# Moving the SBUF start addresses of four groups of tiles by fillers of 32 and 64 bytes, in a four-mixer decoder trunk

## The chip, the cores and the metric

The kernel runs on one core of one Trainium2 chip. The metric is the device time of one execution in microseconds (us). Three runs of the kernel before gave 3079.8, 3082.81 and 3086.07 us; the median is 3082.81 us. The profile is of one more execution, which took 3081.34 us.

## The reference, cut to what matters

The program computes two residual layers over 1024 tokens of 1024 channels in float32. Each layer has a mixer and a gated feed-forward part (ConvFFN) with a hidden width of 2816. The even layer's mixer is a gated DeltaNet with four heads beside a multi-scale pooling; the odd layer's mixer is a dilated sliding-window attention with three groups of eight heads.

```python
for i in range(DEPTH):                       # DEPTH = 2
    mod = (cs @ ada_w[i] + ada_b[i])[:, None, :]
    sh_m, sc_m, g_m, sh_f, sc_f, g_f = jnp.split(mod, 6, axis=-1)
    hm = rms_norm(x, norm_mix[i]) * (1.0 + sc_m) + sh_m
    y = even_mixer(hm, ...) if i % 2 == 0 else odd_mixer(hm, ...)
    x = x + g_m * y
    hf = rms_norm(x, norm_ffn[i]) * (1.0 + sc_f) + sh_f
    x = x + g_f * conv_ffn(hf, ffn_w_up[i], ffn_conv_w[i], ffn_conv_b[i], ffn_w_down[i])
```

## The kernel before, in words

**Split products.** The large products run in the rounded type float32r, one pass each. A weight tile of 128 partitions x 512 float32 (2 KiB in each partition) comes by DMA into `raw` or `wr`; ScalarE copies it into `whi` (the rounded weight) and VectorE or GpSimd writes the rest, weight minus rounded weight, into `wlo`. Activations are split in the same way into `hh` and `hl` or `oh` and `ol`. `mm3` (lines 204 to 208) then adds three matmuls into PSUM: high by high (L206), high weight by activation rest (L207), weight rest by high activation (L208). Here the weight block of 128 columns is stationary and 512 (at the very end 256) columns of activation move. In the odd layer's projections (`tproj`, L1354 to L1356) it is the other way round: a 128-column slice of `hh` or `hl` is stationary and 512 columns of `whi` or `wlo` move. In a profile row such as `sp<-oh,whi` the name behind the arrow is the moving operand, and the one behind the comma the stationary operand.

**Pools.** SBUF tiles come from pools, laid out one behind the other in the address space of a partition: `cst` (constants), `pw` (`raw` 4 buffers, `whi` 9, `wlo` 9), `pb` (24 buffers of 4 KiB, the large tiles: `x`, `hh`, `hl`, `oh`, `ol`, `xr`, `wr`, `v`, `sb`, `big` and others), `pt` (8 buffers `t2k` of 2 KiB and small ones), and one pool per stage: `pe` for the even mixer, `pf0` and `pf1` for the feed-forward parts, `po` for the odd mixer. Buffers of one tag follow each other at multiples of 32 bytes, and nearly all tiles of 512 bytes and more have sizes that are multiples of 128, so all buffers of such a tag share the start's remainder modulo 128 (`stg` and `ld` of the odd mixer, 2080 and 3120 bytes, do not). `fill(pool, bytes)` allocates a tile that no instruction uses, so that what follows in the pool starts later.

**Order.** The order of the instructions on each engine is the order of the Python program. Generators `weave` a chain of dependent small steps with dense matmul work. Semaphores guard every buffer. No planner chooses by address. SP issues nearly all DMAs, a few come from GpSimd and ScalarE.

The stages in time: about 0 to 540 us even mixer, to 1260 us its feed-forward part (from 985 us on the down projection), to about 2375 us odd mixer, to the end its feed-forward part.

Of the kernel before, what the change touches and what calls it, by code (L numbers as in the profile page):

```python
# [34 lines left out]
def trunk(ctx, tc, x, c, ada_w, ada_b, norm_mix, norm_ffn, ev_w_in, ev_w_out, gdn_conv_w,  # L35
# [6 lines left out]
    pw = pool("pw")  # L42
    pb = pool("pb")
# [8 lines left out]
    def nm(s):  # L52
        n_ids[0] += 1
        return f"{s}_{n_ids[0]}"
# [13 lines left out]
    def raw_tile():  # L68
        return pw.tile([P, HALF], F32, tag="raw", name=nm("raw"), bufs=4)
# [4 lines left out]
    def fill(pl, size):  # L74

        pl.tile([P, size // 4], F32, name=nm("fill"))
# [100 lines left out]


    lo_eng = [nc.gpsimd]
    last_w = [None]  # L180

    def split(dst_hi, dst_lo, src, eng):
        nc.scalar.activation(dst_hi, src, AF.Copy)  # L183
        eng.tensor_tensor(out=dst_lo, in0=src, in1=dst_hi, op=ALU.subtract)  # L184

    def granule(src, shape=None):
        raw = raw_tile()
        last_w[0] = nc.sync.dma_start(raw if shape is None else raw.rearrange(shape[0], **shape[1]), src)
        hi = pw.tile([P, HALF], F32R, tag="whi", name=nm("whi"), bufs=9)
        lo = pw.tile([P, HALF], F32R, tag="wlo", name=nm("wlo"), bufs=9)  # L190
        split(hi, lo, raw, lo_eng[0])
        return hi, lo

    def unit_c(w, c0):

        blocks = []
        for g in range(0, KT, 4):
            hi, lo = granule(w[g * P:(g + 4) * P, c0:c0 + P].rearrange("(k p) c -> p k c", p=P),
                             ("p (k c) -> p k c", dict(k=4)))
            blocks += list(zip(blk4(hi), blk4(lo)))  # L200
        return blocks
# [18 lines left out]
    def update(rows, hid, gate, xt, order, wide=False, done=None):  # L220

        wb = []
        for r in rows:
            g = [granule(r[:, q * HALF:(q + 1) * HALF]) for q in range(2)]
            wb.append([(a, b) for hi, lo in g for a, b in zip(blk4(hi), blk4(lo))])
        n = len(rows)
        ps = None
        for o, hf in order:
            s = HS[hf]
            if wide:  # L230
                ps = mm_ps() if hf == 0 else ps
                p = ps[:, s]
            else:
                p = s_ps()
            for i in range(n):
                mm3(p, wb[i][o], hid[i][hf], i == 0, i == n - 1)
                if i < n - 1:
                    yield 3 * MM
            if not wide:
                nc.vector.scalar_tensor_tensor(out=xt[o][:, s], in0=p, scalar=gate[:, o:o + 1], in1=xt[o][:, s],  # L240
                                               op0=ALU.mult, op1=ALU.add)
            elif hf:
                nc.vector.scalar_tensor_tensor(out=xt[o], in0=ps, scalar=gate[:, o:o + 1], in1=xt[o],
                                               op0=ALU.mult, op1=ALU.add)
            if done:
                done(o, hf)
            step_back()
            yield 3 * MM
# [192 lines left out]
    def even():  # L441
# [7 lines left out]
        zs, res = {}, {}  # L449

        with tc.tile_pool(name="pe", bufs=1) as pe:
            fill(pe, 64)

            def et(tag, bufs, shape=(P, HALF)):
                return tmp(tag, shape, bufs, pl=pe)
# [262 lines left out]
            def dense():  # L718
# [37 lines left out]
                with tc.issue_after(last_w[0].ins):  # L756
                    o01 = [[granule(osp[i][:, s]) for s in HS] for i in range(2)]
                    res["x"] = reload(xs[0])
# [328 lines left out]
    def ffn(l, xt, h, vec, acc, vec_next):  # L1087
        gate = mod[l][:, 40:48]
        wu, wd = ffn_w_up[l], ffn_w_down[l]
        with tc.tile_pool(name=f"pf{l}", bufs=1) as pf:  # L1090
            fill(pf, 64)

            def taps(t, src, j, dst, frm):

# [195 lines left out]
    def odd(xt, h, vec, acc):  # L1290
# [3 lines left out]
        spill(xs[1], xt)  # L1294
        lo_eng[0] = nc.vector
        with tc.tile_pool(name="po", bufs=1) as po:
            fill(po, 64)

            def et(tag, bufs, shape=(P, HALF), dt=F32):
                return tmp(tag, shape, bufs, dt, pl=po)  # L1300
# [397 lines left out]
    with tc.tile_pool(name="pa", bufs=1) as pa[0]:  # L1698
        xt, h, vec, acc = even()
        xt, h, vec, acc = ffn(0, xt, h, vec, acc, lambda: norm_vec(1, 0))  # L1700
    xt, h, vec, acc = odd(xt, h, vec, acc)
    ffn(1, xt, h, vec, acc, None)


# [27 lines left out]
```

## Time and profile before

| | |
|---|---|
| median of three runs | 3082.81 us (3079.8 to 3086.07) |
| profiled execution | 3081.34 us, its span from first to last instruction 3079.6 us |
| TensorE matmul busy | 2967.4 us, 96% of the span, 14346 matmuls |
| TensorE weight load busy | 2446.9 us, 79% |
| VectorE, ScalarE, GpSimd busy | 2018.0, 1074.1, 972.2 us (66%, 35%, 32%) |
| DMA queue q1 (the SP queue carries nearly all of it) | 300.55 MB, 31.0% of 16 engines |
| mean granted TensorE clock | 0.986 |

Matmuls are pipelined: the duration of one (0.39 us for 512 columns) overlaps the next, and its end is modelled. What sets TensorE's pace is the distance from one start to the next, which the timeline shows. A busy share of 96% therefore says that TensorE hardly idles; it says nothing on how fast it runs.

### The profile page before, as it was taken

The page shows a single profiled execution, that of the slowest core. Times are in us where ns is not written, and L with a number is a line of the kernel's source. Part 1 is how long each engine was busy: PE and PEld are TensorE (multiplying, and loading weights), DVE is VectorE, ACT ScalarE, POOL GpSimd, SP SyncE. Part 2 cuts the span into 40 slices and gives each one's busy share as a digit, 9 for nine tenths or more (in the row PEclk, how much of TensorE's full clock was granted, in tenths as well). Part 3 has the DMA queues.
Part 4 walks back from the last instruction along what each step waited for, and adds up shares of the span by engine and source line. Part 5 has one row for each costly group of instructions (what it writes and reads, how often), then busy time and mean ns, then how long its engine had stood idle before and what let it go on. Part 6 is the DMA issues. An engine that isn't in the chain of part 4 may idle for free.

```text
span 3079.6 us, 40200 instructions
## 1 busy us (share of the span) xinstructions
PE 2967.4 (96%) x14346; PEld 2446.9 (79%) x14346; DVE 2018.0 (66%) x3877; ACT 1074.1 (35%) x2170; POOL 972.2 (32%) x727
## 2 busy tenths in 40 slices
PE   6999999899999899999999999999999899999999
PEld 4777878678888777788888878888877788888888
DVE  7877745987777877754445646354687877776554
ACT  4434422433333211323333333324343433333210
POOL 4412323555555543200000010000022655555540
PEclk8999999999999999999999999999999999999999
DMA  7523323253323753221313242313243222224321
GB/s 248 145 63 99 96 91 121 72 158 110 110 86 106 240 164 114 106 86 61 106 61 114 65 149 72 115 37 117 68 163 114 85 89 83 82 82 168 110 90 59
DMA packets 275010, 331.46 MB, mean 108 GB/s; under 512 B 27411, under 2 KB 194426, under 8 KB 274810
## 3 DMA queue, kind: packets, MB, share of 16 engines
q1 hardware_dynamic: 266810, 300.55, 31.0%
q0 software_dynamic: 7040, 25.17, 2.4%
q10 hardware_dynamic: 960, 3.18, 0.3%
q8 instruction: 113, 1.85, 0.2%
q14 instruction: 87, 0.71, 0.1%
HBM read 251.82 MB, written 77.00 MB: 107 GB/s over the span
## 4 chain that ended last, share of the span: by engine, by line
PE 72%; DVE 7%; DMA 3%; issue 2%; POOL 1%; ACT 1%; SPq 0%; POOLq 0%; DVEq 0%; ACTq 0%
PE sp L206 11%; PE sp L207 11%; PE sp L208 11%; PE mm L1356 8%; PE mm L1354 8%; PE mm L1355 8%; PE mm L206 3%; PE mm L207 3%; PE mm L208 3%; PE sp L1550 2%; PE sp L1506 2%; PE sp L1386 1%; DVE ada_acc L276 1%; PE sp L1539 1%; DMA raw<-in_ada_w_dram 1%
## 5 line engine op out<-in xcount | busy, mean ns | idle before, releaser
L1354 PE MATMUL mm<-whi,hh 128*128 128x512 f32 x1152 | 482.7, 419 | 0.0
L1356 PE MATMUL mm<-whi,hl 128*128 128x512 f32 x1152 | 452.7, 393 | 0.0
L1355 PE MATMUL mm<-wlo,hh 128*128 128x512 f32 x1152 | 451.6, 392 | 0.0
L184 POOL TENSOR_TENSOR wlo<-raw,whi 128x512 fp32r<-128x512 f32 x190 | 257.0, 1367 | 544.5 <-ACT whi L183 463.8
L183 ACT ACTIVATE whi<-raw 128x512 fp32r<-128x512 f32 x334 | 208.4, 630 | 389.6 <-PE sp L207 163.0
L240 DVE SCALAR_TENSOR_TENSOR xr<-sp,mod,xr 128x512 f32<-128x512 f32 x336 | 248.0, 747 | 135.6 <-PE sp L208 135.2
L206 PE MATMUL sp<-oh,whi 128*128 128x512 f32 (+1 forms) x832 | 315.6, 379 | 20.2 <-DVE xr L240 14.2
L207 PE MATMUL sp<-ol,whi 128*128 128x512 f32 (+1 forms) x832 | 311.1, 374 | 0.0
L208 PE MATMUL sp<-oh,wlo 128*128 128x512 f32 (+1 forms) x832 | 311.0, 374 | 0.0
L206 PE MATMUL mm<-hh,whi 128*128 128x512 f32 x736 | 299.6, 407 | 8.8 <-DVE ft L1098 6.8
L207 PE MATMUL mm<-hl,whi 128*128 128x512 f32 x736 | 294.0, 399 | 3.2 <-POOL hl L377 1.6
L208 PE MATMUL mm<-hh,wlo 128*128 128x512 f32 x736 | 293.1, 398 | 0.0
L184 POOL TENSOR_TENSOR wlo<-t2k,whi 128x512 fp32r<-128x512 f32 x160 | 228.8, 1443 | 159.0 <-ACT whi L183 120.7
L1451 POOL DMA_DIRECT2D vd<-v x24 | 17.6, 735 | 771.9 <-ACT v L1448 379.4
L1356 PEld LDWEIGHTS mm<-whi,hl 128*128 128x128 f32 x1152 | 216.6, 188 | 48.0
L1355 PEld LDWEIGHTS mm<-wlo,hh 128*128 128x128 f32 x1152 | 217.9, 189 | 37.2 <-DVE wlo L184 0.2
L1354 PEld LDWEIGHTS mm<-whi,hh 128*128 128x128 f32 x1152 | 217.5, 189 | 36.1
L184 POOL TENSOR_TENSOR wlo<-wr,whi 128x512 fp32r<-128x512 f32 x114 | 177.5, 1559 | 161.5 <-ACT whi L183 158.6
L206 PEld LDWEIGHTS sp<-oh,whi 128*128 128x128 f32 x832 | 157.0, 189 | 55.7 <-DVE xr L240 21.6
L208 PEld LDWEIGHTS sp<-oh,wlo 128*128 128x128 f32 x832 | 157.1, 189 | 28.2
L207 PEld LDWEIGHTS sp<-ol,whi 128*128 128x128 f32 x832 | 157.1, 189 | 26.3
L206 PEld LDWEIGHTS mm<-hh,whi 128*128 128x128 f32 x736 | 140.8, 191 | 38.8 <-issue 10.7
(395 smaller groups left out, 6147.4 us busy)
## 6 DMA issues: line engine op xcount, KB each, us to landing
raw<-in_ada_w_dram SPq DMA_DIRECT2D x160, 256.0 KB
wr<-in_ffn_w_up_dram SPq DMA_DIRECT2D x76, 512.0 KB
raw<-in_od_w_in_dram SPq DMA_DIRECT2D x144, 256.0 KB
hid<-ft SPq DMA_DIRECT2D x44, 512.0 KB
raw<-in_ffn_w_down_dram SPq DMA_DIRECT2D x88, 256.0 KB
big<-hid SPq DMA_DIRECT2D x44, 512.0 KB
xr<-xs SPq DMA_DIRECT2D x32, 512.0 KB
os<-stg SPq DMA_DIRECT2D x96, 130.0 KB
```

Of the source, the lines that this page charges most:

```text
L183: nc.scalar.activation(dst_hi, src, AF.Copy)
L184: eng.tensor_tensor(out=dst_lo, in0=src, in1=dst_hi, op=ALU.subtract)
L206: nc.tensor.matmul(ps, wh, mh, start=first, stop=False)
L207: nc.tensor.matmul(ps, wh, ml, start=False, stop=False)
L208: nc.tensor.matmul(ps, wl, mh, start=False, stop=last)
L240: nc.vector.scalar_tensor_tensor(out=xt[o][:, s], in0=p, scalar=gate[:, o:o + 1], in1=xt[o][:, s], op0=ALU.mult, op1=ALU.add)
L276: nc.vector.scalar_tensor_tensor(out=acc, in0=raw, scalar=cs[:, k:k + 1], in1=acc, op0=ALU.mult, op1=ALU.add)
L1354: nc.tensor.matmul(p, hh, wh, start=(k == 0), stop=False)
L1355: nc.tensor.matmul(p, hh, wl, start=False, stop=False)
L1356: nc.tensor.matmul(p, hl, wh, start=False, stop=(k == KT - 1))
L1506: nc.tensor.matmul(ps[:, at:at + len(ks) * P], qks[i][0][:, hh, blk * P:(blk + 1) * P], qks[i][1][:, hh, ks[0] * P:(blk + 1) * P], start=T ...
L1550: nc.tensor.matmul(ps[:, j * P:(j + 1) * P], pTs[n][:, a0 + c * P:a0 + (c + 1) * P], vb(kb, hh), start=(c == 0), stop=(c == len(ks) - 1))
```

## The change

Two fillers are added and three are halved. No instruction is added, removed or moved: on each of TensorE, VectorE, ScalarE, GpSimd and SP the rows of the program are the same before and after, in the same order and with the same operands, when the running numbers in tile names and the line numbers (5 more behind the edit) are left aside.

```diff
+    placed = []
+    fill(pb, 64)
     last_w = [None]
@@ granule
         hi = pw.tile([P, HALF], F32R, tag="whi", name=nm("whi"), bufs=9)
+        if not placed:
+            placed.append(True)
+            fill(pw, 32)
         lo = pw.tile([P, HALF], F32R, tag="wlo", name=nm("wlo"), bufs=9)
@@ even, ffn, odd: the stage pools pe, pf, po
-            fill(pe, 64)
+            fill(pe, 32)
-            fill(pf, 64)
+            fill(pf, 32)
-            fill(po, 64)
+            fill(po, 32)
```

What this does to the addresses, read from the two built programs (start of a tile within a partition, remainder modulo 128; behind it the remainder modulo 256 of the first buffer):

| tiles | before | after |
|---|---|---|
| `raw` | 32 (160) | 32 (160) |
| `whi` | 32 (160) | 32 (160) |
| `wlo` | 32 (160) | 64 (192) |
| large tiles of `pb` | 32 (160) | 0 (0) |
| `t2k` | 32 (160) | 0 (0) |
| `g2`, `ft`, `ext`, `qkT`, `bm` and the triangles, first in their stage pools | 32 (160) | 96 (224) |
| `lt`, `zc`, `yv`, `st`, `rhs`, `qs`, further on in `pe` | 0 | 64 |
| `ada_acc` | 96 | 64 |
| `wp` | 96 | 32 |
| `ident`, `ones`, `cols` in `cst` | 0 | 0 |

Before, nearly every operand of the large products starts at 32 modulo 128; after, the moving and the stationary operand of every large product start at different remainders. `wab` and the split DeltaNet outputs are `g2` buffers.

## The prediction

> **What bounds the kernel now.** The page first: its busy shares, the granted clock in 40 slices, and the chain of work that ended last.
>
> ```profile
> span 3079.6 us, 40200 instructions
> PE 2967.4 (96%) x14346; PEld 2446.9 (79%) x14346; DVE 2018.0 (66%) x3877; ACT 1074.1 (35%) x2170; POOL 972.2 (32%) x727
> ...
> PEclk8999999999999999999999999999999999999999
> ...
> PE 72%; DVE 7%; DMA 3%; issue 2%; POOL 1%; ACT 1%; SPq 0%; POOLq 0%; DVEq 0%; ACTq 0%
> ```
>
> TensorE is busy 96% of the span at nearly full clock and carries 72% of the chain; VectorE's 7% are 216 us, DMA's 3% 92 us. An address can act on the time in three ways: through TensorE's pace in the dense stretches, through the duration of a VectorE, ScalarE or GpSimd instruction on the chain, or through a transfer on the chain. So I read the number of large matmuls next, from the groups by line with shapes kept apart (one row of three: the two other lines of a product have the same count).
>
> ```profile
> L1354 PE MATMUL mm<-whi,hh 128*128 128x512 f32 x1152 | 482.7, 419 | 0.0
> L206 PE MATMUL mm<-hh,whi 128*128 128x512 f32 x736 | 299.6, 407 | 8.8 <-DVE ft L1098 6.8 <-DVE big L600 2.0
> L206 PE MATMUL sp<-oh,whi 128*128 128x512 f32 x704 | 278.4, 395 | 20.2 <-DVE xr L240 14.2 <-DVE xr L367 4.9 <-DVE t2k L367 1.1
> L206 PE MATMUL sp<-hh,whi 128*128 128x512 f32 x352 | 137.3, 390 | 0.0
> L206 PE MATMUL sp<-ext,whi 128*128 128x512 f32 x320 | 124.5, 389 | 0.0
> ```
>
> These five groups make 3264 x 3 = 9792 matmuls of 512 columns. Their own durations overlap, so the pace is the distance of starts in the timeline. In the second feed-forward part, with nothing between them:
>
> ```profile
> 2599.81 0.39 PE L207 MATMUL mm<-hl,whi 128*128 128x512 f32 x1
> ...
> 2603.89 0.39 PE L207 MATMUL sp<-ext,whi 128*128 128x512 f32 x1
> ```
>
> ```profile
> 3029.78 0.28 PE L206 MATMUL sp<-oh,whi 128*128 128x256 f32 x1
> ...
> 3032.90 0.28 PE L208 MATMUL sp<-oh,wlo 128*128 128x256 f32 x1
> ```
>
> The first pair has 18 distances between its ends (19 rows, six products and one): 4.08 / 18 = 0.2267 us for 512 columns. The second has 26 (27 rows): 3.12 / 26 = 0.1200 us for 256. The slope is 0.1067 / 256 = 0.417 ns a column, so 512 columns cost 213.3 ns and a fixed rest of 13.3 ns belongs to each matmul whatever its width. The 9792 matmuls at 0.2267 us take 2220 us, 72% of the span: this is what the chain says, and any address effect on TensorE is multiplied by some 10,000. One nanosecond a matmul is 9.8 us, 0.32%. A measurement of this kernel can tell about 0.2%, 6.2 us, from no change, so 0.63 ns a matmul decides.
>
> **The change part by part.** No instruction comes, goes or moves; five fillers shift starts. It removes one thing: that moving and stationary operands, and what the other engines read and write beside them, start at the same remainder (32 modulo 128). The cost or gain is 9792 times a change of the 13.3 ns or of the 0.417 ns slope, plus what the other engines and the transfers do.
>
> *TensorE against the other engines.* If streams of the same remainder got in each other's way, the pace would be worse where the other engines are busy. The windows view has such a stretch:
>
> ```profile
> 600.00:1000.00 400.00, 397.38 (x1747) 328.32 (x1748) 316.29 (x361) 148.32 (x217) 223.25 (x148) 0.99 0.35 111
> ```
>
> The columns are TensorE, its weight loads, VectorE, ScalarE and GpSimd busy, then clock and DMA share. With VectorE busy 79%, ScalarE 37%, GpSimd 56%, 400 us hold 1747 matmuls: 0.2290 us each on average, with the waits and the 128-column ones in it. At most 0.2290 - 0.2267 = 2.3 ns a matmul is there to be won from the neighbours, 22.5 us over 9792, and the largest part of it is other waiting. The timeline row above stands in the same kind of stretch and is already at the 213.3 + 13.3 ns of the quiet last part (0.1200 us per 256 columns comes from 3030 us, where the chain is only TensorE). I take 0.
>
> *Moving against stationary operand.* Here the trace of before has a test of its own, in float32: `lt` starts at 0 and `yv` at 0, while `t2k`, `g`, `v` and `sb` start at 32. The instructions by line (min, median, max in ns):
>
> ```profile
> L935 PEld LDWEIGHTS sp<-t2k,lt x128: 186/192/338, 167.3 to 391.8; 128*128 128x128 f32 x128
> L935 PE MATMUL sp<-t2k,lt x128: 275/275/422, 167.5 to 391.9; 128*128 128x128 f32 x128
> ...
> L942 PEld LDWEIGHTS sp<-g,t2k x128: 186/192/193, 170.3 to 393.7; 128*128 128x128 f32 x128
> L942 PE MATMUL sp<-g,t2k x128: 270/275/377, 170.4 to 393.8; 128*128 128x128 f32 x128
> ...
> L999 PE MATMUL sp<-yv,g x64: 271/275/421, 184.0 to 473.8; 128*128 128x128 f32 x64
> ```
>
> and their distances in the timeline, merged rows of 16:
>
> ```profile
> 314.28 2.00 PE L935 MATMUL sp<-t2k,lt 128*128 128x128 f32 x16
> ...
> 386.78 2.05 PE L942 MATMUL sp<-g,t2k 128*128 128x128 f32 x16 [1.06 <-DVE t2k L937]
> ```
>
> Moving 32 with stationary 0 (L935): (2.00 - 0.275) / 15 = 0.115 us from start to start. Both at 32 (L942): (2.05 - 0.275) / 15 = 0.118. Weight loads have the same median of 192 ns, and moving 0 with stationary 32 (L999) the same 275. So in float32 neither meeting nor missing remainders costs a nanosecond that the medians show. But these are 128 columns at 0.115 us, 0.9 ns a column, half the pace of the rounded type; a conflict could hide in that slack. The trace has no large float32r product with different remainders. Bounds for it: at best the whole 13.3 ns goes, 9792 x 13.3 = -130 us; at worst every one of them runs at the slowest steady pace that the trace shows, behind interleaved float32 work in the odd layer:
>
> ```profile
> 2262.82 0.39 PE L1355 MATMUL mm<-wlo,hh 128*128 128x512 f32 x1
> ...
> 2264.43 0.39 PE L1356 MATMUL mm<-whi,hl 128*128 128x512 f32 x1
> ```
>
> Seven distances, 1.61 / 7 = 0.230 us, 3.3 ns above the quiet pace: 9792 x 3.3 = +32 us. Between -130 and +32 I take 0, by the float32 rows, which are the nearest that differ in remainder alone.
>
> *VectorE, ScalarE, GpSimd.* The odd mixer's merge reads `ld` at starts that run through many remainders (its rows have 130 elements), ScalarE's exponentials of the same size read `sb`, always 32:
>
> ```profile
> L1601 ACT ACTIVATE t2k<-ld,me 128x128 f32<-128x128 f32 x64 | 21.4, 393 | 9.6 <-DVE me L1596 8.2 <-DMA ld<-os 1.3
> ...
> L1531 ACT ACTIVATE sb<-sb,neg 128x128 f32<-128x128 f32 x104 | 41.1, 396 | 103.2 <-DVE neg L1529 99.3 <-issue 3.3
> ```
>
> 393 against 396 ns. VectorE's accumulation reads 32 and 96 and writes 96, its residual update stays at 32 (the second operand is PSUM):
>
> ```profile
> L276 DVE SCALAR_TENSOR_TENSOR ada_acc<-raw,cs,ada_acc x140: 731/752/2874, 102.4 to 1194.3; 128x512 f32<-128x512 f32 x140
> ...
> L240 DVE SCALAR_TENSOR_TENSOR xr<-sp,mod,xr x336: 732/750/754, 509.6 to 3022.1; 128x512 f32<-128x512 f32 x168
> ```
>
> Median 752 against 750. Bounds: plus or minus 2 ns in 750 of VectorE's 216 us on the chain is 0.6 us. I take 0.
>
> *Transfers.* `raw` stays where it was, `big`, `xr`, `wr` and `v` now start at a multiple of 256. The longest transfers on the chain of waits in time order are
>
> ```profile
> 993.25 6.21 DMA xr<-xs
> 999.52 10.18 DMA big<-hid
> ```
>
> both into large tiles. The trace shows no transfer at another start, so bounds: nothing to, at best, a tenth of the chain's 92 us, -9 us; at worst the same, +9 us. I take 0. [...]
>
> *Sum.* The profiled execution took 3081.34 us (span 3079.6 and 1.7 around it); change 0 + 0 + 0 + 0. The median of the runs lies 1.5 us above the profiled one. I predict 3082 us, with a range of its own of 3076 to 3088.
>
> **The rivals.**
>
> *Faster, TensorE (0.11).* The 13.3 ns are a meeting of the moving and the stationary read on one remainder, and part of them goes. For it: they are fixed per matmul, as a weight load is. Against: the float32 rows show no sign, and a fixed swap cost looks the same. Half of it gone is -65 us, 3017 us.
>
> *Slower, TensorE (0.17).* Equal remainders are the good case: streams that start alike run in step, and after the change the weight load beside each product (192 ns in the float32 rows above, most of the 227) hits the line that the moving operand needs. Place: every product of L206 to L208 and L1354 to L1356. For it: a pace of 0.230 exists. Against: that one follows float32 work. Price: if only the third with `wlo` is hit, 3264 x 3.3 = 11 us, 3093; if all, 32 us, 3114. It decides from 0.63 ns a matmul on.
>
> *Faster, transfers (0.08).* In the stretch at the start of the down projection the transfers are what TensorE waits for:
>
> ```profile
> 985.00:1080.00 95.00, 86.40 (x368) 68.15 (x366) 79.25 (x95) 23.03 (x30) 50.96 (x29) 0.98 0.71 237
> ```
>
> DMA share 0.71, TensorE idle 8.6 us. With aligned large tiles this gap goes: 3074. Against: half of the stretch's transfers are `raw`, which does not move. [...]
>
> *Slower, the stage pools (0.08).* The tiles from 32 to 96 (`ft`, `ext`, `g2`, `qkT`) meet others at 0 and 32 in VectorE's two-operand instructions. If each of some 290 on the chain (216 us at 0.75) cost 30 ns more, that is 9 us, 3091. Against: L276 with 32 and 96 shows 2 ns.
>
> That the change doesn't move the addresses is excluded by the built program.
>
> **How the numbers follow.** No change has 0.56, faster 0.11 + 0.08 = 0.19, slower 0.17 + 0.08 = 0.25. The range takes in the transfer and stage-pool cases, and the slower TensorE case to nearly its full 32 us; on the fast side it reaches to -22.5 us, the bound of what the neighbours can cost. That is 3060 to 3112, and leaves out most of the faster TensorE case.
>
> **What would show it.** The timeline of quiet stretches: 18 distances in 4.08 us again, or not; a step between L206, L207 and L208 there would show which pairing matters (`wlo` at 64, `ext` at 96). 1747 matmuls in a 400 us stretch like 600 to 1000. The medians of L276, L240, L184 and L183. The DMA pieces at 985 to 1080. I am wrong if the pace changes by more than 0.6 ns, whichever way.

## The result, and the profile after

The changed kernel takes 3119.02 us in the median of four runs (3112.35 to 3121.88), the kernel before 3084.44 us beside it (four runs, 3079.8 to 3088.15): a ratio of 1.0109, with an interval of 1.0092 to 1.0125. It is slower by 34.6 us, where no change was the forecast. The profiled execution took 3119.16 us with a span of 3117.4 us, 37.8 us more than the span before.

The page of the kernel after, its busy shares, its clock and its chain by engine:

```profile
span 3117.4 us, 40200 instructions
PE 3008.4 (97%) x14346; PEld 2442.7 (78%) x14346; DVE 2029.4 (65%) x3877; ACT 1075.6 (35%) x2170; POOL 973.3 (31%) x727
...
PEclk8999999999999999999999999999999999999999
...
PE 72%; DVE 7%; DMA 3%; issue 2%; POOL 1%; ACT 1%; SPq 0%; DVEq 0%; POOLq 0%; ACTq 0%
```

The shares tell almost nothing: the same instructions, the same clock digits, the same chain. TensorE's busy time is 41 us longer, at a busy share that was already 96%. The pace shows it. A quiet stretch of the second feed-forward part, to set beside the stretch of before at 2599.81 us (only the first and the last row of 25):

```profile
2599.27 0.39 PE L211 MATMUL sp<-hh,whi 128*128 128x512 f32 x1
...
2604.87 0.39 PE L211 MATMUL mm<-hh,whi 128*128 128x512 f32 x1
```

24 distances in 5.60 us are 0.2333 us; before it was 0.2267. The step between the lines that the prediction asked for is there too: the distance from the third product (L213, with `wlo`) to the next start is 234.9 ns on average, that from each of the first two 231.8; before, it was 227.5 against 227.3 and 227.2. The windows of the same times as before have fewer matmuls (1747 and 368 were in them before), at a clock that is no lower, and TensorE idles in them at most 0.8 us more (3.4 and 9.4 us, before 2.6 and 8.6):

```profile
600.00:1000.00 400.00, 396.65 (x1705) 320.00 (x1706) 311.44 (x352) 147.30 (x215) 223.28 (x148) 1.00 0.33 105
...
985.00:1080.00 95.00, 85.58 (x363) 66.10 (x362) 78.37 (x90) 26.76 (x33) 48.08 (x28) 1.00 0.67 224
```

Setting the starts of all TensorE rows of the two traces against each other, one by one, gives the account. A "dense" pair is a large product of 512 columns and whatever TensorE starts next, when that comes within 0.26 us in both traces.

| stage (time before, us) | dense pairs | their distances, us | a pair, ns | all the rest, us | sum, us |
|---|---|---|---|---|---|
| even mixer (to 540) | 1083 | +4.4 | +4.1 | -4.1 | +0.3 |
| first feed-forward (to 1260) | 2843 | +16.3 | +5.7 | -0.9 | +15.4 |
| odd mixer (to 2375) | 3427 | +8.8 | +2.6 | -3.9 | +4.9 |
| second feed-forward | 2734 | +16.9 | +6.2 | +0.4 | +17.3 |
| all | 10087 | +46.5 | +4.6 | -8.6 | +37.9 |

The pace of the large products accounts for all of it and more; the other distances, waits among them, took 8.6 us back, nearly all in the two mixers. The medians of the other engines' instructions that the prediction named did not move:

```profile
L281 DVE SCALAR_TENSOR_TENSOR ada_acc<-raw,cs,ada_acc x140: 732/752/2973, 104.6 to 1208.4; 128x512 f32<-128x512 f32 x140
...
L245 DVE SCALAR_TENSOR_TENSOR xr<-sp,mod,xr x336: 729/750/753, 509.4 to 3060.8; 128x512 f32<-128x512 f32 x168
...
L186 POOL TENSOR_TENSOR wlo<-raw,whi x190: 1261/1294/1833, 21.2 to 3060.5; 128x512 fp32r<-128x512 f32 x190
...
L185 ACT ACTIVATE whi<-raw x334: 611/632/682, 20.5 to 3059.8; 128x512 fp32r<-128x512 f32 x167
```

Medians of 752 and 750 ns, the figures of before; L186 and L185 were L184 and L183 (1296 and 632 ns there). VectorE's busy time as a whole rose by 11.4 of 2018 us, in small amounts over many groups, and GpSimd's 160 splits of `t2k` went from 1293 to 1316 ns; TensorE's pace alone more than fills the account above.

### The profile page after: what moved, and what is told of

Read it like the earlier page. It is cut to its first block, busy times and chain, and to the rows that moved or that the text cites. A ratio compares the mean times of both kernels' runs of the same rounds, so it can differ in the third digit from the quotient of the medians.

```text
span 3117.4 us, 40200 instructions
## 1 busy us (share of the span) xinstructions
PE 3008.4 (97%) x14346; PEld 2442.7 (78%) x14346; DVE 2029.4 (65%) x3877; ACT 1075.6 (35%) x2170; POOL 973.3 (31%) x727
## 4 chain that ended last, share of the span: by engine, by line
PE 72%; DVE 7%; DMA 3%; issue 2%; POOL 1%; ACT 1%; SPq 0%; DVEq 0%; POOLq 0%; ACTq 0%
PE sp L211 11%; PE sp L213 11%; PE sp L212 11%; PE mm L1359 8%; PE mm L1361 8%; PE mm L1360 8%; PE mm L213 3%; PE mm L211 3%; PE mm L212 3%; PE sp L1555 2%; PE sp L1511 2%; PE sp L1391 1%; PE sp L1544 1%; DVE ada_acc L281 1%; DMA big<-hid 1%
## 5 line engine op out<-in xcount | busy, mean ns | idle before, releaser
L186 POOL TENSOR_TENSOR wlo<-raw,whi 128x512 fp32r<-128x512 f32 x190 | 254.3, 1353 | 559.4 <-ACT whi L185 456.6
L185 ACT ACTIVATE whi<-raw 128x512 fp32r<-128x512 f32 x334 | 208.6, 630 | 405.2 <-PE sp L212 174.3
L211 PE MATMUL sp<-oh,whi 128*128 128x512 f32 (+1 forms) x832 | 318.3, 383 | 21.2 <-DVE xr L245 15.7
L213 PE MATMUL sp<-oh,wlo 128*128 128x512 f32 (+1 forms) x832 | 316.0, 380 | 0.0
L212 PE MATMUL sp<-ol,whi 128*128 128x512 f32 (+1 forms) x832 | 313.6, 377 | 0.0
L211 PE MATMUL mm<-hh,whi 128*128 128x512 f32 x736 | 300.4, 408 | 7.2 <-DVE ft L1103 6.4
L212 PE MATMUL mm<-hl,whi 128*128 128x512 f32 x736 | 295.9, 402 | 2.6 <-DVE hl L382 1.6
L213 PE MATMUL mm<-hh,wlo 128*128 128x512 f32 x736 | 296.7, 403 | 0.0
L186 POOL TENSOR_TENSOR wlo<-t2k,whi 128x512 fp32r<-128x512 f32 x160 | 232.2, 1465 | 165.3 <-ACT whi L185 160.3
L186 POOL TENSOR_TENSOR wlo<-wr,whi 128x512 fp32r<-128x512 f32 x114 | 178.1, 1565 | 168.2 <-ACT whi L185 162.6
L211 PEld LDWEIGHTS sp<-oh,whi 128*128 128x128 f32 x832 | 156.7, 188 | 60.8 <-DVE xr L245 23.1
L212 PEld LDWEIGHTS sp<-ol,whi 128*128 128x128 f32 x832 | 156.6, 188 | 31.5
L213 PEld LDWEIGHTS sp<-oh,wlo 128*128 128x128 f32 x832 | 156.2, 188 | 31.5
L211 PEld LDWEIGHTS mm<-hh,whi 128*128 128x128 f32 x736 | 139.8, 190 | 38.7 <-issue 9.1
```

What stands on the lines that cost most here:

```text
L211: nc.tensor.matmul(ps, wh, mh, start=first, stop=False)
L212: nc.tensor.matmul(ps, wh, ml, start=False, stop=False)
L213: nc.tensor.matmul(ps, wl, mh, start=False, stop=last)
```

## The experiments

After the result there were these questions: is it the value of a start or the difference between moving and stationary operand; with which period does it repeat; which group of tiles carries it; and why is the loss 4.6 ns a pair, when the worst of the bounds was 3.3. Remainders are modulo 256 from here on. Before, `raw`, `whi`, `wlo`, the large tiles, `t2k` and the stage pools were all at 160; after, `raw` and `whi` are at 160, `wlo` at 192, large tiles and `t2k` at 0, stage pools at 224. In all runs of the whole kernel but `e4` and `i1` the tile `cols`, of which 359 columns are used, has 384 columns instead of 512, which makes room for fillers. The diffs are against the kernel before, with only the lines that matter (`...` where others lie between), and leave that line out. Where a mean is given without a row, it is the mean distance from the start of a large product to the next start, where that is at most 0.26 us, over the whole trace.

### Everything equal, at another value

```diff
+    fill(pw, 96)          # ahead of raw: every group moves to 0
```

> All of raw, whi, wlo, the large tiles, t2k and the stage pools' first tiles start at 0 modulo 128 (and modulo 256): equal remainders as before, another value. Theory R (the pace of a large product depends on whether its moving and its stationary operand start at the same remainder): quiet pace 0.2267 us as before, time 3084 within 0.3%. Theory A (an operand's own remainder matters, 32 is a good one and 0 or 64 a bad one): every large product at 0.231 us or more, 3115 us or more.

Measured: 3083.93 us against 3083.02, ratio 1.0001 (0.9992 to 1.001). The timeline in the second feed-forward part, 24 distances in 5.44 us, 0.2267 us:

```profile
2600.26 0.39 PE L208 MATMUL mm<-hh,whi 128*128 128x512 f32 x1
...
2605.70 0.39 PE L208 MATMUL sp<-ext,whi 128*128 128x512 f32 x1
```

All starts moved by 96 bytes and nothing changed. So 160 is not a good value of its own; what counts is whether the operands differ.

### Large tiles at 0 with the weights left at 160

```diff
+    fill(pb, 96)
+    fill(pt, 32)
```

> Only the large tiles go from 32 to 0; whi, wlo, t2k and the stage pools stay at 32. Theory R: products with a large tile moving and whi or wlo stationary at 0.2315 to 0.232 us, both alike now; products with ext moving back at 0.2267; the odd layer's projections about 3 ns slower than before; by the size these had in the changed kernel, 3105 to 3115 us. Theory W (it was the shift of wlo): no change, 3084.

`whi` and `wlo` stay equal to each other; large tiles are 96 bytes from them, `t2k` and the stage pools (at 32) 128. Measured: 3129.6 us, ratio 1.0154 (1.0137 to 1.0172), 46.6 us above the before of that comparison, more than the whole change. All products are slow: 231.5 to 234.9 ns with large tiles, 233.1 to 233.3 with `ext`, 233.0 to 234.3 in the odd layer's projections. `wlo` need not differ from `whi` for a loss. The expectation had `ext` back at 0.2267 us, because it went by remainders modulo 128, where `ext` lies level with the weights; that did not come true, and the size was above its 3105 to 3115 us.

### Only the stage pools apart

```diff
-            fill(pe, 64)
...
-            fill(pf, 64)
...
-            fill(po, 64)
```

> Only the stage pools go from 32 to 96. Theory R: only products with ext, g or qkT moving (some 1150 matmuls) go from 0.2267 to 0.231 us, +4 to +6 us, 3088 to 3090 us; all others stay at 0.2267. Theory V (VectorE or ScalarE work on tiles of different remainders is what costs): medians of those instructions rise, more than 6 us.

`ext`, `g2` and `qkT` are at 96, everything else at 160. Measured: 3092.02 us (seven runs), ratio 1.0026 (1.0013 to 1.0039). Products with `ext`, then 256-column products of the last part, whose `oh` and `ol` also lie in the `ext` buffers:

```profile
2599.60 0.39 PE L207 MATMUL sp<-ext,whi 128*128 128x512 f32 x1
...
2602.40 0.39 PE L207 MATMUL sp<-hh,whi 128*128 128x512 f32 x1
...
3070.04 0.28 PE L207 MATMUL sp<-oh,whi 128*128 128x256 f32 x1
...
3071.74 0.28 PE L207 MATMUL sp<-oh,whi 128*128 128x256 f32 x1
```

Twelve distances in 2.80 us are 0.2333 us for `ext`; all other large products average 228.4 ns where they had 228.1, and 227 in the median as before. 960 products with `ext` and 192 with `g2` and `qkT` at 6.6 ns more are 7.6 us, against 9.0 measured between the medians. The stage pools do cost something, through TensorE and not through VectorE (its instructions take 1.5 us less in sum, and L276 has its median of 752 ns as before). The other pair was a surprise: 15 distances in 1.70 us are 0.1133 us for 256 columns, faster than the 0.1200 of before.

### Half of 256

```diff
+    fill(pb, 128)
```

> The large tiles, t2k and the stage pools lie 128 bytes further on against whi and wlo: still 32 modulo 128, but 32 and 160 modulo 256. Theory R with a period of 128 bytes: pace 0.2267, 3084 us. Theory R with a period of 256: all large products slower, 3110 us or more.

Large tiles, `t2k` and stage pools are at 32, the weights at 160: equal modulo 128, not modulo 256. Measured: 3122.56 us, ratio 1.013 (1.0115 to 1.0145), 24 distances in 5.58 us, 0.2325 us:

```profile
2598.86 0.40 PE L208 MATMUL mm<-hh,whi 128*128 128x512 f32 x1
...
2604.44 0.39 PE L208 MATMUL sp<-hh,whi 128*128 128x512 f32 x1
```

The remainder modulo 128 is not the one that counts.

### A map of the pace

The trunk is left out and the output is a copy of `x`: TensorE alone multiplies 32 blocks at a time, four weight blocks in turn, with the moving operand (or the weights, or both) shifted.

```diff
+        for i in range(count):
+            a = st + i % 4 * P
+            nc.tensor.matmul(p[:, :n], wt[:, a:a + P], mt[:, mv:mv + n], start=(i == 0), stop=(i == count - 1))
```

> Only matmuls of one weight tile and one moving tile, both starting at a multiple of 256, without any other engine at work; the trunk is left out and the output is a copy of x. Groups of 32 matmuls of 128x512 in the rounded type, with 4 weight blocks in turn; the moving operand starts 0, 4, ... 256 bytes further on; then the weights, then both; then with 256, 384 and 128 columns, and in float32. Theory R256 (TensorE's two own reads meet, with a period of 256 bytes): 0.2267 us at 0 and at 256 and where both move together, 0.229 to 0.237 us at 32 to 224; with 256 columns 0.120 at 0 and 0.113 to 0.119 elsewhere; float32 without a difference. Theory N (other engines' reads or writes are what the moved tiles meet): 0.2267 us at every offset, since no other engine runs.

Each row is 32 matmuls (16 of the float32 ones); the number in the name is the shift in bytes. The pace is (second column - 0.39) / 31 (0.28 for 256 columns), good to about 0.3 ns:

```profile
38.86 7.42 PE L67 MATMUL moving000x<-m,w 128*128 128x512 f32 x32
...
68.47 7.57 PE L67 MATMUL moving016x<-m,w 128*128 128x512 f32 x32
...
98.15 7.63 PE L67 MATMUL moving032x<-m,w 128*128 128x512 f32 x32
...
157.60 7.48 PE L67 MATMUL moving064x<-m,w 128*128 128x512 f32 x32
...
239.66 7.42 PE L67 MATMUL moving108x<-m,w 128*128 128x512 f32 x32
...
276.93 7.62 PE L67 MATMUL moving128x<-m,w 128*128 128x512 f32 x32
284.39 7.83 PE L67 MATMUL moving132x<-m,w 128*128 128x512 f32 x32
...
515.80 7.43 PE L67 MATMUL moving256x<-m,w 128*128 128x512 f32 x32
...
552.50 7.62 PE L67 MATMUL weight064x<-m,w 128*128 128x512 f32 x32
...
612.11 7.63 PE L67 MATMUL weight192x<-m,w 128*128 128x512 f32 x32
...
634.51 7.44 PE L67 MATMUL weight240x<-m,w 128*128 128x512 f32 x32
...
678.16 7.45 PE L67 MATMUL both128x<-m,w 128*128 128x512 f32 x32
...
714.59 4.00 PE L67 MATMUL half000x<-m,w 128*128 128x256 f32 x32
...
729.75 3.79 PE L67 MATMUL half064x<-m,w 128*128 128x256 f32 x32
...
759.86 3.80 PE L67 MATMUL half192x<-m,w 128*128 128x256 f32 x32
...
838.21 7.03 PE L67 MATMUL full064x<-mraw,wraw 128*128 128x512 f32 x16
845.07 7.03 PE L67 MATMUL full128x<-mraw,wraw 128*128 128x512 f32 x16
```

At 0 and 256 it is 226.8 ns, at 32 and 128 233.3, at 64 228.8, at 132 240.0. With both moved by 128 it is 227.7, with a few slow matmuls at the group's start and 226.7 behind them. No other engine computes beside these groups, and the mean granted clock of the run is 1.00: the loss appears with TensorE's own two operands alone. At 256 bytes the pace of 0 is back, but it is no smooth function of the distance: offsets such as 28, 60, 108, 156, 236 and 240 cost nothing (226.7 to 227.1 ns), and 4 bytes beside them the loss is up to 13 ns (240 ns at 244). No offset is faster than 226.6.

Nor does the distance alone fix the pace. Weights moved by 192 stand to the moving operand as in `moving064`, modulo 256, and take 233.4 ns where that took 228.8; weights moved by 240 stand as in `moving016`, and take 227.3 where that took 231.6. What holds in every row of 512 columns is that equal remainders settle at 226.7. With one weight block throughout instead of four in turn the pace at 32 and 64 bytes is the same, 233 and 229 ns.

For 256 columns an unequal pair can be the better one: 120.0 at 0, 113.2 at 64, 113.4 at 192. Products of 384 columns take 173.4 ns at 0, 32 and 64 and up to 176.7 at 192. Products of 128 columns take 111.6 to 111.7 ns at every offset tried, and the float32 rows ("full", at 64 and 128) do not differ at all.

### Only the rests of the weights apart

```diff
+    fill(pb, 224)
...
+            fill(pw, 32)          # between whi and wlo
```

> Only wlo starts 32 bytes further on (modulo 256: 192, all other operands of the large products at 160). Theory own (a matmul is slow when its own weights differ from its moving operand): L206 and L207 at 0.2267, the third line of mm3 at 0.229 to 0.233; in the odd layer the line that moves wlo slower. About 3552 + 1152 matmuls by 3 to 6 ns: +14 to +28 us, 3097 to 3111 us. Theory next (a matmul is slow when the weights that load beside it differ from it): the second line slow and the third at 0.2267, the same time.

Only `wlo` is at 192, everything else at 160. Measured: 3123.86 us against 3084.69, ratio 1.0127 (1.011 to 1.0144). The timeline: 24 distances in 5.60 us, 0.2333 us, with 0.23, 0.24, 0.23 in the order of the three lines:

```profile
2598.77 0.40 PE L211 MATMUL mm<-hh,whi 128*128 128x512 f32 x1
...
2600.17 0.40 PE L211 MATMUL sp<-ext,whi 128*128 128x512 f32 x1
2600.40 0.40 PE L212 MATMUL sp<-ext,whi 128*128 128x512 f32 x1
2600.64 0.39 PE L213 MATMUL sp<-ext,wlo 128*128 128x512 f32 x1
...
2604.37 0.40 PE L211 MATMUL sp<-hh,whi 128*128 128x512 f32 x1
```

One operand in three differs, and all three products are slow: 232.4, 238.2 and 228.9 ns on average for L211, L212 and L213. That no line stays at 226.7 speaks against a cost that sits with the product's own pair and as much against one that sits with the next pair. The map's run had this case for TensorE alone, in groups where every third weight (`v`) lies 32 bytes off:

```profile
862.06 0.39 PE L90 MATMUL trio032x<-m,v 128*128 128x512 f32 x1
862.29 0.63 PE L90 MATMUL trio032x<-m,w 128*128 128x512 f32 x2
862.76 0.39 PE L90 MATMUL trio032x<-m,v 128*128 128x512 f32 x1
```

Three take 0.70 us, and one by one they settle at 233, 239 and 228 ns, the pattern of the kernel. The loss of 39 us by `wlo` alone exceeds that of all five fillers. It is not quite a part of the change, though: here `wlo` lies 32 bytes above the large tiles (192 against 160), in the change 64 below them (192 against 256).

### Large tiles at the offset that is nearly free

```diff
+    fill(pb, 64)
+    fill(pt, 192)
```

> The large tiles alone lie 64 bytes further on modulo 256 (224 against 160 for whi, wlo, t2k and the stage pools). Theory M (the map of the microbenchmark carries over): products with a large tile moving at 0.2288 us instead of 0.2267, about 6050 x 2.1 ns = 13 us; the odd layer's projections, where the moving operand lies 64 below, at most 3 to 6 ns up, half of it seen as in the changed kernel, 6 us; together 3100 to 3105 us. Theory U (any inequality modulo 256 costs the same): as with 96 or 128 bytes, 3120 to 3130 us.

Large tiles are at 224, all else at 160. Measured: 3112.59 us, ratio 1.0094 (1.0079 to 1.0109), between what the map's 228.8 ns gave and what a uniform loss gave. The timeline has two paces:

```profile
2600.30 0.39 PE L209 MATMUL mm<-hh,whi 128*128 128x512 f32 x1
...
2605.79 0.40 PE L209 MATMUL sp<-ext,whi 128*128 128x512 f32 x1
...
2608.56 0.40 PE L209 MATMUL mm<-hh,whi 128*128 128x512 f32 x1
```

24 products with large tiles take 5.49 us, 0.2288 each, as in the map. The next 12, with `ext`, take 2.77 us, 0.2308 each, although `ext` and both weights lie equal at 160. A pair that is equal is slow behind pairs that are not. So here the pace does not follow from the product's own pair. This and `e8` called for one more run.

### How long a disturbance lasts

The trunk is left out again. Twelve matmuls with the moving operand d bytes off ("apart"), twelve at the same remainder ("equal"), six times, then 64 equal ones; and one, two or four in 24 at 128 bytes.

```diff
+    for d in (32, 64, 96, 128, 192):
+        for r in range(6):
+            chunk(f"apart{d:03d}r{r}x", d // 4, 12)
+            chunk(f"equal{d:03d}r{r}x", 0, 12)
+        chunk(f"settle{d:03d}x", 0, 64)
```

> The trunk is left out (the output is a copy of x); TensorE alone multiplies 512-column float32r blocks, four weight blocks in turn, one core, no other engine at work. Groups alternate six times: 12 matmuls with the moving operand d bytes away from the weights (apart), then 12 with both at the same remainder modulo 256 (equal), and after the six a settling group of 64 equal ones; the same in the order of a split product (high weight, high weight, rest); and 1, 2 or 4 matmuls at 128 bytes in each 24. It is to explain why the ext products of the run with the large tiles 64 bytes up took 230.8 ns each although weight and ext lay equal. Theory carry (a disturbed sequence needs some matmuls of equal operands to settle, as the groups with both operands moved together showed over 8): the equal groups of 12 take 228 to 232 ns a matmul on average, the first ones 229 to 236 and the last ones near 227, the settling group of 64 under 228 on average; one matmul in 24 at 128 bytes costs 10 to 40 ns more than the 6.6 of its own. Theory own (a matmul's time follows from its own pair or the next one alone, so something else in the kernel slowed ext, such as the DMA that fills it): the equal groups take 226.6 to 227.2 from their second matmul on, and one matmul in 24 costs under 10 ns.

The merged rows for d = 64 and 128:

```profile
113.43 2.93 PE L69 MATMUL apart064r5x<-m,w 128*128 128x512 f32 x12
116.20 2.93 PE L69 MATMUL equal064r5x<-m,w 128*128 128x512 f32 x12
118.97 14.67 PE L69 MATMUL settle064x<-m,w 128*128 128x512 f32 x64
...
209.05 2.95 PE L69 MATMUL apart128r5x<-m,w 128*128 128x512 f32 x12
211.84 2.90 PE L69 MATMUL equal128r5x<-m,w 128*128 128x512 f32 x12
214.58 14.67 PE L69 MATMUL settle128x<-m,w 128*128 128x512 f32 x64
```

From start to start, the equal group behind 64 bytes takes 118.97 - 116.20 = 2.77 us, 0.2308 us a matmul: the number of `ext` in the run before. One by one its distances are 234, 231, 233, 236, 224, 231, 236, 228, 233, 231, 226 and 227 ns: ten matmuls until it is back. Behind 128 bytes it is three, behind 192 five, behind 32 and 96 seven to eight. The 64 that follow are at 226.7 throughout. In the order of a split product, with two moving and two weight tiles, the groups at 64 bytes take the same, 230.2 apart and 230.8 equal. The expectation that one matmul in 24 at 128 bytes would cost 10 to 40 ns more was wrong: it takes 234.2 ns itself, and the next is already at 225 to 226. So the carry-over is shown, its length depends on the offset, and a single foreign matmul at 128 bytes leaves none, while two in a row do: three equal ones behind them take 232, 232 and 231 ns.

### Moving the last part alone

```diff
+            def ext_up(dt=F32R, name="ext"):
+                return pf.tile([P, T + 64 * l], dt, tag="ext", name=nm(name), bufs=8)[:, 16 * l:T + 16 * l]
...
-            last = row_blocks(wd, js), [from_dram(hid_d[l][j], ext) for j in js], gate, xt
+            last = row_blocks(wd, js), [from_dram(hid_d[l][j], ext_up) for j in js], gate, xt
```

(`ext` itself gets the same longer tiles.)

> The kernel before, with only the moving operands of the last part (256 columns) 64 bytes further on. Theory M: these 384 matmuls at 0.1133 us instead of 0.1200, 2.6 us less, 3080 to 3082 us, if the transposes and VectorE work between them don't hold them up; all else as before. Theory U: slower or the same.

Measured: 3083.95 us (11 runs) against 3084.85, ratio 1.0002 (0.9993 to 1.001). In the last part:

```profile
3029.79 0.28 PE L207 MATMUL sp<-oh,whi 128*128 128x256 f32 x1
...
3033.33 0.28 PE L207 MATMUL sp<-oh,whi 128*128 128x256 f32 x1
```

30 distances in 3.54 us, 0.1180 us instead of 0.1200, not the 0.1132 of the map. On 384 products that is 0.8 us, under what a measurement can tell. Why the kernel gets 118.0 at +64 bytes where it got 113.3 at -64 (`e4`) is open; the map, which starts its weights at 0 and not at 160, has about 113.3 at both (`half064`, `half192`). No version measured beats the kernel before.

## Why the prediction was wrong

**What bounds the kernel** was right, and so was the lever: each nanosecond a large product is about 10 us. The prediction counted 9792 products in its five groups; five smaller groups (`t`, `g`, `qkT` and the two `mm` groups of 64 that have only `whi`/`wlo` or `oh`/`ol` as moving operand) add 352 x 3 = 1056, so there are 10848 large products, and 10087 of them have a dense distance behind them. (Of these 10848, 64 still have equal starts after the change: those that move `whi` against `whi`, both at 160.)

**"Moving against stationary operand", taken as 0, is the step that failed.** Its measured value is +46.5 us in the profiled execution before waits give 8.6 back. It failed in two ways.

First, the value was taken from the float32 rows, on the ground that they alone differ in remainder. In the map float32 products do not react to the offset (the "full" rows at 64 and at 128 take 7.03 us each), nor do products of 128 columns (111.6 to 111.7 ns). The prediction itself named the slack of 0.9 ns a column in which a conflict could hide, and then chose by that row. A test that cannot fail is no evidence.

Second, the upper bound of +32 us was not a bound: the change cost 34.6. The 0.230 us of the odd layer was called the slowest steady pace in the trace. It is not steady: the stretch shown is nine products behind narrower work, about as many as a sequence needs to settle after a disturbance (three to ten in `m2`). The trace of before shows the settling itself. Behind narrower work, the distances from the second, third and fourth large product are on average 231.1 to 232.3 ns, those from the fifth to the tenth 227.4 to 230.6, and those from the eleventh on 226.5 to 227.0. After the change the first three are hardly slower (231.3 to 232.6), and from the eleventh on they are 231 to 234. So the change costs next to nothing on the products that had not settled anyway, and of the odd layer's 339 unbroken sequences of large products 304 have nine or fewer. That is why the odd layer lost only 2.6 ns a pair: its dense distances went from 229.3 to 231.8 ns, those of the second feed-forward part from 226.7 to 232.9. The map has a loss of up to 13.2 ns a matmul, four times the 3.3 of the bound.

**The rival "Slower, TensorE" (0.17)** named what happened: equal remainders are the good case, every product of the five groups is the place, and it decides far above 0.63 ns. The time, 3119 us, is above the 3114 that it gave this case. Two things in it were not borne out: its mechanism of a weight load that hits "the line that the moving operand needs" (no run shows what is hit; offsets of 28 or 108 cost nothing), and its split, by which a third of the price would fall due if only the products with `wlo` are hit. In `e8` a difference in one product of three slows all three (232.4, 238.2 and 228.9 ns). Nor can the loss of 34.6 us be shared out among the groups: the runs with one group moved lost 9 us (stage pools), 39 (rests) and 28 (large tiles), but none of them holds that group at its distance in the change (the stage pools lie 64 bytes below `whi` there and 64 above here, the large tiles 64 above and not 96). The large tiles stand at the change's 96 bytes in `e3`, which moves the stage pools too and lost 46.6. The mis-sized term is the 3.3 ns: in the change it measured 4.6 over all dense pairs, 6.2 in the second feed-forward part.

**"Faster, TensorE" (0.11)** fell for 512 columns: no offset is below 226.6 ns, so the fixed 13.3 ns are not a meeting of equal remainders. Nor do they belong to a matmul "whatever its width": at the prediction's slope 384 columns fit (160.0 + 13.4 = 173.4), but 128 columns would be 53.3 ns and take 111.7. At 256 columns half of it can go (120.0 to 113.2), a case that only the last 384 products have.

**TensorE against the other engines, taken as 0**, is confirmed by the map: with no other engine computing the pace at offset 0 is the same 226.8. **VectorE, ScalarE, GpSimd, taken as 0**, held for the rows it named (752, 750, 1294 and 632 ns), and with it the rival of the stage pools fell as it was put; alone, moved 64 bytes down, the stage pools cost 9 us, but in TensorE. **Transfers, taken as 0**: the 367 matmuls of the window at 985 us leave TensorE idle 9.3 us where it was 7.7, so the rival by which aligned large tiles close that gap fell. The 10.18 us transfer of the prediction took 10.08 us at its new start:

```profile
1008.89 10.08 DMA big<-hid
```

One transfer that is 0.10 us shorter does not show what its start is worth.

## What to carry to other kernels

Let the moving and the stationary operand of float32r products of 512 columns start at the same remainder modulo 256 (226.7 ns a product here, up to 240.0 with unequal starts), and keep it the same for all operands of a sequence: in `e8` one operand in three that differs gave 232.4, 238.2 and 228.9 ns. Read TensorE's pace as the distance of starts in a quiet stretch, because the busy share (96% before, 97% after), the clock (0.986 and 0.989) and the chain (TensorE 72% in both) do not show a pace that is 3% slower (0.2333 us against 0.2267). And take a row as evidence on a suspected cost only if the row could have shown it.

## What was not expected of the hardware

- The pace of 512-column float32r products depends, in the map, on how moving and stationary start lie to each other modulo 256: 226.7 ns when equal, up to 240.0 when not, in no smooth order (moving operand shifted by 28: 226.8; 32: 233.3; 64: 228.8; 128: 233.3; 132: 240.0; 240: 226.7). The distance is not the whole rule: shifting the weights by 192 gives 233.4, not the 228.8 of 64.
- It depends on what ran before: after twelve products at 64 bytes, ten equal ones pass until the pace is back at 226.7 ns; after 128 bytes three.
- With 256 columns an unequal start can be the faster one, 113.2 against 120.0 ns; 128 columns (111.6 to 111.7) and float32 with 512 columns (429 ns) did not react at the offsets tried.
- What in the chip makes the pattern is open: the runs show where it appears, not what collides.
